# 64 unused bytes behind each of the first group's four T tiles: places that step by 64 modulo 256

## The chip, the cores and the metric

The kernel runs on one core of a Trainium2 chip. The metric is the time of one execution on the device, in microseconds. The profile is of one execution on the same core.

## What is computed

One step of a one-layer decoder trunk, for a prompt group of 1024 tokens and a sample group of 8 x 8 = 64 tokens with common weights, 1088 tokens in all, of width 1024, in float32:

```
h = RMSNorm(x)
q, k, v, gu, gv, ga, gb = split(h @ w_in)
A = sliding-window (128) grouped-query attention with per-head sinks
B = gelu(gu) * (W_s[g] LN(gelu(gv)) + b[g])      # 128-position chunks, W_s lower triangular
x = x + (sigmoid(ga) * (A @ w_branch_attn) + sigmoid(gb) * (B @ w_branch_gmlp)) @ w_out
z = RMSNorm(x) @ w_up                            # 1024 -> 2 * 2816
a, b = split(causal depthwise conv of width 3 over z)
x = x + (gelu(a) * b) @ w_down
y = RMSNorm(x)
```

Keys, values, the last rows of z and the normalised gv of the samples are outputs too.

## The kernel before

Every matrix product runs in float32r with both operands split in two: a high part that TensorE takes as it is, and the rest as a low part. A product is the sum of three matmuls, high x high, low x high and high x low. `split` (L39) makes the parts: a cast on ACT, a subtraction on DVE, both under L41.

The tokens stand in two groups. Group 0 has 576 (the 64 samples and 512 of the prompt), group 1 has 512. Two stages, the pair phase (L948, q, k, gu and the gates) and the up projection (L1570 and L1626), multiply pairs of weight tiles by the tokens with a scheme of seven products instead of eight: weights, tokens and outputs are cut into halves, seven sums of weight halves are multiplied by seven sums of token halves, and `Chain.product` (L293) adds or subtracts what comes out (L307 to L331). So for each of the two stages a group has seven sums of token halves for each of four pieces `kk` of the contraction, high and low: the T tiles.

Group 0's T tiles are made by `both_planes` (L258): one tile for each `kk`, 128 partitions x 7 sums x 2 planes (high, low) x 288 columns. `t0_job` (L657) fills them for the pair phase, in the pool `T0h`, and `t0_split` (L1421) for the up projection, in the pool `T0`. In the profile both are named `t`. Group 1's T tiles are separate tiles for high and low, 7 x 256 columns, in the pools `T1h` and `T1`; the profile names them `th` and `tl`.

One product of a chain is twelve matmuls into one PSUM bank, `st` (L305): for each `kk` the moving operand is the high plane with the weights' high part `wh`, the low plane with `wh`, and the high plane with their low part `wl`. Each loads its weights anew, 128 x 128. Where both groups are in work, a product of group 0 (288 columns) is followed by the same product of group 1 (256 columns) with the same weights. Three pairs of the pair phase and three of the up projection (`FEWA`, `FEW`) run on one group alone. The weights come through `Weights` (L72) from the pool `wp`, where each high or low part takes 8 pieces of 128 x 128.

Other stages that the prediction speaks of: `tokens` (L559, matmuls at L523), where the tokens are the weights and the projection's columns the moving operand (`w2h`, `w2l`); `mm3` (L231, matmuls at L238) for the branches and the output projection, with 320, 256 and 512 columns (`s`, `oh`, `ol`, `mh`, `ml`); and the down projection (L1673), with tiles `th`, `tl` of 544 columns taken as 288 and 256.

Pools are stacked from the two ends of on-chip memory. `line(pool, n)` (L246) takes a tile of n bytes for each partition that nothing reads or writes; the kernel has it already at other pools. `T0h` and `T0` are the first of the right side, from the upper end down. Below `T0h` lies `xr`, the staging for the pair phase's T tiles. Below `T0` lies `bt` (L1383): the group's rows `x1g`, `nacc` and two tiles `traw`, of which the sums of group 1's T tiles are made and split (L1491). When `bt` is closed, `c2` with the convolution's state `stc` is opened over its place and loaded by SP (L1595).

The order of the instructions on each engine is the order in which the code issues them, and waits come from the tiles' uses.

Of the kernel before, what the change touches and what calls it, by code (L numbers as in the profile page):

```python
# [34 lines left out]
def layer(tc, a):  # L35
# [13 lines left out]
    with ExitStack() as top:  # L49
# [196 lines left out]
        def line(pool, n):  # L246

            pool.tile([P, n // 4], F32, name=f"gap{next(gaps)}", bufs=1)
# [8 lines left out]

        def both_planes(pool, name):  # L258
            t = pool.tile([P, 7, 2, 288], F32R, name=name)
            return t[:, :, 0], t[:, :, 1]  # L260

        def combine(t4, b11, b12, b21, b22, eng=G):
# [108 lines left out]
        with ExitStack() as ph1:  # L371
# [285 lines left out]
            def t0_job(kk):  # L657
                def go():
                    first, t4, rest = sums_of(0, kk)
                    txa[0][kk] = th, tl = both_planes(t0h, f"t{kk}")  # L660
                    split(th[:, 0], tl[:, 0], first)
                    split(th[:, 1:5], tl[:, 1:5], t4)
                    split(th[:, 5:7], tl[:, 5:7], rest)
                return go
# [756 lines left out]
            def t0_split(kk):  # L1421

                def go():
                    x0, x1, t4 = hx.pop(kk)
                    tx[0][kk] = th, tl = both_planes(t0p, f"t0{kk}")
                    split(th[:, 0], tl[:, 0], x0[:, 0:288])
                    split(th[:, 5:7], tl[:, 5:7], x1.rearrange("p (h c) -> p h c", h=2))
                    split(th[:, 1:5], tl[:, 1:5], t4)
                return go
# [483 lines left out]
```

## Time and profile before

| | us |
|---|---|
| median of 3 runs | 1518.02 (1517.09 to 1523.28) |
| profiled execution | 1517.25 |
| its span, first to last instruction | 1515.5 |
| TensorE (PE) busy in the span | 1500.0 |
| weight loads (PEld) busy | 1459.7 |
| VectorE (DVE) busy | 1177.5 |
| ScalarE (ACT) busy | 848.7 |
| GpSimd (POOL) busy | 265.5 |

The mean granted clock of TensorE is 0.998. Weight loads overlap matmuls, and matmuls overlap one another: the duration of one runs from its first column to the end of its passage through the array, while the next one has long begun. The pace of a stream is therefore the distance from start to start, as the timeline shows it. In the lists of groups the columns are the line, the engine and the operation, output <- inputs by the program's names, the shape and the count, then busy time and the mean duration in ns of one, and the idle time before them. In the lists for one tile three numbers give the shortest, the median and the longest duration in ns.

### The profile page before, as it was taken

Reading aid. Unit: us, or ns where it says so; the run is one execution under the profiler, and the core shown is the slowest. Engines: PE = TensorE matmul, PEld = TensorE weight load, DVE = VectorE, ACT = ScalarE, POOL = GpSimd, SP = SyncE. Lnnn points to the kernel's source line nnn. Section 1 sums busy time; section 2 is a strip of 40 time slices with the busy share of each in tenths; the row PEclk is TensorE's granted clock in tenths of the full one; section 3 lists DMA queues with packets and bytes.
Section 4 is the critical chain, followed back from the end, with each engine's and each line's share of the span. In section 5 each row is a group of like instructions: output and inputs, shape, how many; then the busy total and the mean of one; then the engine's idle time right before and its main releaser. Section 6 shows DMA issues by size and latency. Waiting matters only on the chain.

```text
span 1515.5 us, 30104 instructions
## 1 busy us (share of the span) xinstructions
PE 1500.0 (99%) x11528; PEld 1459.7 (96%) x11528; DVE 1177.5 (78%) x1897; ACT 848.7 (56%) x1767; POOL 265.5 (18%) x382
## 2 busy tenths in 40 slices
PE   9999999999999999999999999999999999999997
PEld 9999999999998989988989999999999999999997
DVE  7799876755576877979568988898899888785686
ACT  7557676654465675764344555655555556353452
POOL 0001000110030222220134322332132222000002
PEclk9999999999999999999999999999999999999999
DMA  7688446864679757439988333332232216973463
GB/s 253 221 280 271 153 159 222 252 213 143 240 251 282 221 163 251 152 138 304 338 286 273 134 116 115 122 121 95 110 126 106 105 61 235 366 254 97 117 183 123
DMA packets 135231, 289.88 MB, mean 191 GB/s; under 512 B 15536, under 2 KB 36848, under 8 KB 135088
## 3 DMA queue, kind: packets, MB, share of 16 engines
q1 hardware_dynamic: 134944, 287.96, 56.4%
q8 instruction: 90, 1.47, 0.4%
q14 instruction: 53, 0.43, 0.1%
q10 hardware_dynamic: 144, 0.01, 0.0%
HBM read 198.97 MB, written 90.92 MB: 191 GB/s over the span
## 4 chain that ended last, share of the span: by engine, by line
PE 83%; DVE 6%; ACT 4%; DMA 3%; issue 2%; POOL 1%; SPq 0%; POOLq 0%; ACTq 0%; DVEq 0%
PE st L305 45%; PE dn L1673 13%; PE mm L238 13%; PE st L523 6%; PE po L1222 2%; PE sc L1171 1%; DVE wl L41 1%; PE pt L1198 1%; DMA v<-gvd 1%; ACT wh L41 1%; PE mx L805 1%; DMA vnd<-v 1%; ACT s L1188 1%; DMA kd<-q 0%; DVE tl L41 0%
## 5 line engine op out<-in xcount | busy, mean ns | idle before, releaser
L305 PE MATMUL st<-t,wh 128*128 128x288 f32 x2128 | 429.8, 294 | 0.8 <-ACT kn L286 0.8
L305 PEld LDWEIGHTS st<-t,wh 128*128 128x128 f32 x2128 | 337.3, 188 | 1.9 <-ACT kn L286 1.0
L305 PE MATMUL st<-t,wl 128*128 128x288 f32 x1064 | 314.2, 295 | 0.0
L305 PE MATMUL st<-th,wh 128*128 128x256 f32 x1064 | 297.9, 280 | 1.0 <-ACT k L284 0.9
L305 PE MATMUL st<-tl,wh 128*128 128x256 f32 x1064 | 296.3, 278 | 0.0
L305 PE MATMUL st<-th,wl 128*128 128x256 f32 x1064 | 295.1, 277 | 0.0
L305 PEld LDWEIGHTS st<-th,wh 128*128 128x128 f32 x1064 | 200.7, 189 | 2.3 <-ACT k L284 1.8
L305 PEld LDWEIGHTS st<-th,wl 128*128 128x128 f32 x1064 | 200.7, 189 | 0.0
L305 PEld LDWEIGHTS st<-t,wl 128*128 128x128 f32 x1064 | 200.2, 188 | 0.0
L305 PEld LDWEIGHTS st<-tl,wh 128*128 128x128 f32 x1064 | 199.8, 188 | 0.0
L1673 PE MATMUL dn<-th,wh 128*128 128x288 f32 (+1 forms) x616 | 176.9, 287 | 1.0 <-ACT zb L331 0.6
L1673 PE MATMUL dn<-tl,wh 128*128 128x288 f32 (+1 forms) x616 | 176.2, 286 | 0.0
L1673 PE MATMUL dn<-th,wl 128*128 128x288 f32 (+1 forms) x616 | 175.2, 284 | 0.2 <-DVE wl L41 0.2
L41 ACT CAST wh<-wraw 128x512 fp32r<-128x512 f32 (+2 forms) x188 | 129.5, 701 | 79.2 <-DMA wraw<-wt 27.0
L41 DVE TENSOR_TENSOR wl<-wraw,wh 128x512 fp32r<-128x512 f32 (+2 forms) x188 | 148.8, 804 | 28.0 <-ACT wh L41 25.7
L41 ACT CAST wh<-ws 128x512 fp32r<-128x512 f32 x168 | 102.5, 621 | 93.9 <-PE st L305 60.3
L41 DVE TENSOR_TENSOR wl<-ws,wh 128x512 fp32r<-128x512 f32 x168 | 117.8, 712 | 46.9 <-ACT wh L41 46.2
L1673 PEld LDWEIGHTS dn<-th,wh 128*128 128x128 f32 x616 | 115.6, 188 | 1.4 <-ACT zb L331 0.9
L1673 PEld LDWEIGHTS dn<-th,wl 128*128 128x128 f32 x616 | 115.9, 188 | 0.4 <-DVE wl L41 0.4
L1673 PEld LDWEIGHTS dn<-tl,wh 128*128 128x128 f32 x616 | 115.7, 188 | 0.0
L41 ACT CAST th<-traw 128x544 fp32r<-128x544 f32 (+1 forms) x85 | 54.6, 643 | 48.3 <-PE dn L1673 34.9
L523 PE MATMUL st<-w2h,hh 128*128 128x256 f32 x288 | 79.9, 279 | 0.9 <-ACT w2h L41 0.4
(275 smaller groups left out, 3181.8 us busy)
## 6 DMA issues: line engine op xcount, KB each, us to landing
wraw<-wt SPq DMA_DIRECT2D x137, 512.0 KB
traw<-td SPq DMA_DIRECT2D x77, 272.0 KB
td<-za SPq DMA_DIRECT2D x22, 544.0 KB
q<-qd SPq DMA_DIRECT2D x16, 512.0 KB
upd<-hl SPq DMA_DIRECT2D x14, 512.0 KB
td<-t SPq DMA_DIRECT2D x11, 544.0 KB
wpart<-wt SPq DMA_DIRECT2D x22, 256.0 KB
qd<-q SPq DMA_DIRECT2D x8, 576.0 KB
```

The source lines that it names most:

```text
L41: for x in (S.copy(hi, src), V.tensor_sub(lo, src, hi.bitcast(F32))):
L238: PE.matmul(ps[:, lo:lo + c1 - c0], u[:, k, :], v[:, c0:c1], start=(k == 0 and i == 0), stop=(k == nk - 1 and i == 2))
L305: PE.matmul(ps, u[:, kk, :], v, start=first and kk + i == 0, stop=kk == 3 and i == 2, skip_group_check=True)
L523: PE.matmul(ps, u[:, lo:lo + P], v[:, k, :], start=k + i == 0, stop=k == KD - 1 and i == 2)
L805: PE.matmul(ps[:, P * i:P * i + P], vn[:, i], late["wst"][:, c, :], start=True, stop=True)
L1171: PE.matmul(ps[:, h, o0:256], q, kst[kv][:, e, k0:cur + P], start=e == 0, stop=e == 1)
L1188: S.activation(s[:, h], s[:, h], AF.Exp, bias=nm[:, h:h + 1], accum_out=dn[:, h:h + 1])
L1198: PE.transpose(pt[:, h * P:h * P + P], s[:, h, 0:P], ident)
L1222: PE.matmul(po, v[:, kv, :], t, start=e == 0, stop=last)
L1673: PE.matmul(place(m, e), u[:, m, :], v[:, lo:hi], start=new and i + k == 0 and (e == 0 or m % 2 == 0), stop=i == NU - 1 and k == 2, skip_g ...
```

## The change

Behind each tile that `both_planes` makes, 64 bytes for each partition are left unused. `both_planes` is called by `t0_job` and by `t0_split`, so this holds in the pair phase and in the up projection.

```diff
         def both_planes(pool, name):
             t = pool.tile([P, 7, 2, 288], F32R, name=name)
+            line(pool, 64)
             return t[:, :, 0], t[:, :, 1]
```

`line` is as before:

```
        def line(pool, n):
            pool.tile([P, n // 4], F32, name=f"gap{next(gaps)}", bufs=1)
```

## The prediction

> **What bounds the kernel now.** I read the page first: the busy times, the chain that ended last, and the costliest groups.
>
> ```profile
> span 1515.5 us, 30104 instructions
> PE 1500.0 (99%) x11528; PEld 1459.7 (96%) x11528; DVE 1177.5 (78%) x1897; ACT 848.7 (56%) x1767; POOL 265.5 (18%) x382
> ...
> PE st L305 45%; PE dn L1673 13%; PE mm L238 13%; PE st L523 6%; PE po L1222 2%; PE sc L1171 1%; DVE wl L41 1%; PE pt L1198 1%; DMA v<-gvd 1%; ACT wh L41 1%; PE mx L805 1%; DMA vnd<-v 1%; ACT s L1188 1%; DMA kd<-q 0%; DVE tl L41 0%
> ...
> L305 PE MATMUL st<-t,wh 128*128 128x288 f32 x2128 | 429.8, 294 | 0.8 <-ACT kn L286 0.8
> ...
> L305 PE MATMUL st<-t,wl 128*128 128x288 f32 x1064 | 314.2, 295 | 0.0
> L305 PE MATMUL st<-th,wh 128*128 128x256 f32 x1064 | 297.9, 280 | 1.0 <-ACT k L284 0.9
> L305 PE MATMUL st<-tl,wh 128*128 128x256 f32 x1064 | 296.3, 278 | 0.0
> L305 PE MATMUL st<-th,wl 128*128 128x256 f32 x1064 | 295.1, 277 | 0.0
> ```
>
> PE is busy 99% of the span, and L305, the product of a chain, is 45% of the chain that ended last. So nothing has to be waited for less: the time changes if PE's matmuls follow each other at another pace, and hardly otherwise. The groups named `t` read the four T tiles of the first group: 2128 + 1064 = 3192 matmuls of 288 columns, twelve to a product (four tiles, three matmuls each), 266 products. Those named `th`, `tl` read the second group's tiles, 3 x 1064 = 3192 of 256 columns. The mean of one (294 ns) is not the pace, because matmuls overlap in the array. The pace stands in the timeline, from start to start. A product of both chains near the end of the up projection:
>
> ```profile
> 1236.35 0.28 PE L305 MATMUL st<-th,wh 128*128 128x256 f32 x1
> ...
> 1236.94 0.28 PE L305 MATMUL st<-th,wl 128*128 128x256 f32 x1
> ...
> 1237.62 0.28 PE L305 MATMUL st<-th,wl 128*128 128x256 f32 x1
> 1237.74 0.42 PE L305 MATMUL st<-t,wh 128*128 128x288 f32 x2
> ...
> 1239.19 0.29 PE L305 MATMUL st<-t,wl 128*128 128x288 f32 x1
> 1239.32 0.28 PE L305 MATMUL st<-th,wh 128*128 128x256 f32 x1
> ```
>
> The twelve matmuls on T tiles go from 1237.74 to 1239.32: 1.58 us, 132 ns each. All 3192 take 3192 x 0.132 = 421 us, 28% of the span. The twelve of the second group take 1237.74 - 1236.35 = 1.39 us. Their first five need 0.59 us, 118 each, the last seven (1236.94 to 1237.74) 0.80 us, 114 each. So a run of 256 columns starts slowly behind a run of 288 and then settles. The duration follows the pace, 294 at 132 and 276 at 113 to 114, always some 162 above it, so durations can be compared in place of paces. The spread by tile:
>
> ```profile
> L305 PE MATMUL st<-t,wh x2128: 290/294/401, 110.5 to 1259.9; 128*128 128x288 f32 x194
> ...
> L305 PE MATMUL st<-t,wl x1064: 290/295/298, 110.8 to 1260.0; 128*128 128x288 f32 x178
> ...
> L305 PE MATMUL st<-th,wh x1064: 276/276/387, 145.5 to 1271.4; 128*128 128x256 f32 x178
> ```
>
> Minimum, median, maximum: matmuls of one shape (the `wl` row, where none waited) go from 290 to 298. That is all there is for a change of places to move.
>
> **The change, part by part.** It adds a name without an instruction behind each T tile. Engine by engine, the built programs have the same instructions in the same order. A T tile is 7 x 2 x 288 x 4 = 16,128 bytes, 63 x 256, so all four begin at one place modulo 256, which in the built program is 224. The high plane of every product is at 224 (a step of 2304 bytes is 9 x 256), the low plane 1152 bytes on, at 96. The weights' `wh` and `wl` are at 32 for every tile. With 64 bytes more the tiles are at 224, 32, 96 and 160, their low planes at 96, 160, 224 and 32. Everything stacked below them (`xr`, `bt`) moves by 256 bytes and keeps its place modulo 256. Nothing else moves.
>
> *Pace of the 3192 matmuls of 288 columns.* No row shows them at 32 or 160. Bounds from the rows above: if each ran at the minimum, 290 in place of 294, the gain is 4 ns x 3192 = 12.8 us; at the maximum, 298 in place of 295, the loss is 3 x 3192 = 9.6 us. In between, the nearest rows are matmuls of the same shape at another place, and others whose place differs:
>
> ```profile
> L1673 PE MATMUL dn<-th,wh 128*128 128x288 f32 x308 | 91.5, 297 | 0.3 <-ACT wh L41 0.3
> L1673 PE MATMUL dn<-tl,wh 128*128 128x288 f32 x308 | 91.1, 296 | 0.0
> L1673 PE MATMUL dn<-th,wl 128*128 128x288 f32 x308 | 90.1, 292 | 0.2 <-DVE wl L41 0.2
> ...
> L1673 PE MATMUL dn<-tl,wh 128*128 128x256 f32 x308 | 85.1, 276 | 0.0
> ...
> L238 PE MATMUL mm<-mh,wl 128*128 128x512 f32 x64 | 24.9, 389 | 0.0
> ...
> L238 PE MATMUL mm<-oh,wl 128*128 128x320 f32 x64 | 19.9, 311 | 0.0
> ...
> L238 PE MATMUL mm<-mh,wl 128*128 128x320 f32 x64 | 19.7, 308 | 0.0
> ```
>
> In the down projection the 288 columns of both planes begin at 96: (297 + 296 + 292) / 3 = 295.0, against (2 x 294 + 295) / 3 = 294.3 here. The 320 columns of `oh` begin at 224 and those of `mh` at 96: 311 and 308, of which part is the fuller phase in which the former run. The 512 columns of `mh` begin at 32, the very place of the weights, and cost (389 - 276) / 256 = 0.44 ns for each column above 256, no more than the (389 - 308) / 192 = 0.42 above 320. So three places, 96, 224 and 32, show paces alike within 1 to 3 ns. I take 0, with 1 ns either way (3.2 us) as the likely error, and keep -12.8 and +9.6 as ends. The fourth place, 160, is shown for no stream with weights at 32.
>
> The Trainium skill speaks against any effect, in "SBUF — State Buffer", section "SBUF: two separate sides": "PE, ACT, and DVE's dedicated pair never wait on anyone." By it the sum is 0 here, as I take it. The trace neither shows that nor refutes it, but 290 to 298 for one shape at a granted clock of 1.00 is a spread for which the rule has no place. The skill's "TensorE: Matmul & The Clock Gate", section "Back-to-back issue gap", gives columns / 2.4 + 2.5 ns: 122.5 for 288 columns, an estimate 9.5 below the measured 132, or 30 us over 3192. Since no matmul of this shape here comes near it, it is not an end of the range.
>
> *Settling of the 256 columns behind them.* Settled is 276. The means 280, 278 and 277 give (4 + 2 + 1) x 1064 = 7.4 us that unsettled matmuls cost now. In the down projection 256 columns follow 288 too and run at 276 to 277 from the first on. So the gain can be 7.4. The other end is a run of 256 columns that never settles, which the token projection (L523) has, its operands at one place throughout:
>
> ```profile
> 70.00 0.28 PE L523 MATMUL st<-w2l,hh 128*128 128x256 f32 x1
> ...
> 71.42 0.28 PE L523 MATMUL st<-w2l,hh 128*128 128x256 f32 x1
> ...
> 428.00:451.00 23.00, 23.00 (x206) 1.00 0.88 311
> ```
>
> Twelve matmuls in 1.42 us, 118.3 each, while 23.0 us of the second group's alone hold 206, with both that reach over the edges (113 each). The cost would be (118.3 - 113.3) x 3192 = 16.0, less the 7.4 already paid: +8.6 us. I take 0: the matmul ahead of the run still ends in the same chain, and nothing in these rows says towards which end its new place pushes.
>
> *Two new waits.* The load of `stc` (L1595) now also waits for the last split of the second group's tiles, whose staging tile has moved 256 bytes down into it.
>
> ```profile
> 845.45 0.42 SPq L1595 DMA_DIRECT2D stc<-stc  x1
> 848.57 0.33 SPq L1584 DMA_DIRECT2D zd<-zb  x1
> ...
> 845.92 0.93 DVE L41 TENSOR_TENSOR tl<-traw,th 128x512 fp32r<-128x512 f32 x1
> ...
> 852.11 0.62 POOL L1566 COPY za<-stc 128x18 f32<-128x18 f32 x1 [4.58 <-DVE wl L41]
> ```
>
> The split ends at 846.85, so the issue goes from 845.45 to about 846.9. Behind it on SP stands the store of `zb` at 848.57, which waits for a later DVE instruction anyway, and the first reader on POOL comes at 852.11. Cost 0; if that cover were gone, 1.4 us. On POOL one later copy out of `za` (L1551) also waits for ACT, at a point where ACT's last use of the old tile is some 14 us past. Cost 0.
>
> **The sum.** The profiled execution took 1517.25 us, its span 1515.5 and 1.75 around it: 1517.25 + 0 + 0 + 0. The median of the runs is 1518.02, 0.77 higher, so I say 1518.0. The likely case's own range is the 3.2 us above with half the settling term (3.7): 1511 to 1525.
>
> **The rivals.** *The runs fall into step* (faster). A duration of 290 exists, as the minimum shows, and a regular step of places could keep it. In full that is 12.8 + 7.4 = 20.2 us, 1497.8; half of it, 1507.9. For it: all slower paces come without a named wait. Against it: 224, 96 and 32 look alike in the rows, and within a tile the two planes stay 128 apart, so the sequence remains irregular. It counts as faster from 7.6 us on, say all of the settling or 2.4 ns of each 288.
>
> *The second group's runs no longer settle* (slower). Place: the first 256 columns behind the fourth tile, which now ends at 160 + 1152, that is 32, and no longer at 96, modulo 256. Price +8.6, and with 1 ns on each 288 +3.2 more: 1518.0 + 11.8 = 1529.8. It decides as soon as the settling takes over eleven of twelve matmuls in place of five. For it: a run at 118 keeps itself up over dozens of matmuls at L523. Against it: in the down projection such runs settle at once, behind 288 columns at yet another place.
>
> *The change does nothing to PE*: the places matter to no engine, and the time is 1517.25 to 1518.02. That lies inside the forecast and has 0.2 of its chance.
>
> **How the numbers follow.** What a measurement of this kernel can tell from no change is about 0.5%, 7.6 us. Forecast (within that) 0.50; in step 0.24; not settling, or a slower pace of the 288 columns, 0.26. The range takes in the half of the faster rival and nearly all of the slower one: 1507 to 1529, with some 0.1 left out at either side.
>
> **What would show it.** Right: the `t` rows again at 294 and 295, the mean of `th,wh` at 280, twelve T matmuls in 1.58 us, the `stc` load 1.4 us later and POOL's first copy where it was. Faster would show as `t` rows near 290 or `th,wh` near 276; slower as `th` and `tl` rows near 281. I am wrong altogether if time appears at PE as idle time behind DVE, ACT or DMA, since no instruction has changed its order.

## The result and the profile after

The changed kernel takes 1513.39 us (median of 6 runs, 1511.22 to 1515.95), the kernel before beside it 1520.96 us (6 runs, 1517.09 to 1523.28). The ratio is 0.9953, with a 95% interval from 0.9936 to 0.9971: a gain of 4.4 to 9.7 us, which is small but is not nothing. The profiled execution took 1511.66 us.

The page of the kernel after, with the busy times and the costliest groups (busy us, mean ns of one, then idle time before them; a line added in `both_planes` makes L305 to L306):

```profile
span 1509.9 us, 30105 instructions
PE 1492.6 (99%) x11528; PEld 1452.6 (96%) x11528; DVE 1176.0 (78%) x1897; ACT 849.6 (56%) x1767; POOL 269.8 (18%) x382
...
L306 PE MATMUL st<-t,wh 128*128 128x288 f32 x2128 | 428.5, 294 | 2.3 <-ACT kn L287 1.7
...
L306 PE MATMUL st<-t,wl 128*128 128x288 f32 x1064 | 312.5, 294 | 0.0
L306 PE MATMUL st<-th,wh 128*128 128x256 f32 x1064 | 295.4, 278 | 0.7 <-ACT k L285 0.6
L306 PE MATMUL st<-tl,wh 128*128 128x256 f32 x1064 | 294.1, 276 | 0.0
L306 PE MATMUL st<-th,wl 128*128 128x256 f32 x1064 | 293.8, 276 | 0.0
```

The span is 5.6 us shorter and PE's busy time 7.4 us less, with as many matmuls. What became shorter are the rows of the **second** group, `th` and `tl`, whose tiles the change does not touch: 280, 278, 277 are now 278, 276, 276. The rows named `t`, whose tiles did move, went from 294 and 295 to 294 and 294.

The timeline of the kernel after shows how, in the same stretch of the up projection as in the prediction (start and duration in us):

```profile
1230.62 0.28 PE L306 MATMUL st<-th,wh 128*128 128x256 f32 x1
...
1231.19 0.28 PE L306 MATMUL st<-th,wl 128*128 128x256 f32 x1
...
1231.98 0.42 PE L306 MATMUL st<-t,wh 128*128 128x288 f32 x2
...
1233.43 0.29 PE L306 MATMUL st<-t,wl 128*128 128x288 f32 x1
1233.56 0.28 PE L306 MATMUL st<-th,wh 128*128 128x256 f32 x1
```

The first five of the second group's twelve now take 1231.19 - 1230.62 = 0.57 us, 114 each, where they took 0.59, 118 each. The last seven keep 0.79 (0.80 before). The first group's twelve take 1.58 us as before.

The timeline shows 10 ns; the trace has single ns. So below I count the **twelve** of a product from the start of its first matmul to the start of the next product, as a mean over all products in which nothing waited (some 204 of the first group behind one of the second, 218 the other way round). Before: 1580.9 and 1391.8 ns. After: 1576.7 and 1365.5 ns. Twelve settled matmuls of 256 columns take 1360. Summed over all start-to-start distances below 150 ns, the first group's matmuls take 418.1 us before and 416.8 after, the second group's 366.9 and 361.1: both chains together 785.1 and 778.0, 7.1 us less. The distances behind all other matmuls sum to 711.1 and 711.7 us, and the 41 longer ones within the chains to 11.4 and 12.3. So 7.1 us less and 0.6 and 0.9 more make the 5.6 us by which the span is shorter.

The new wait on SP stands in the timeline of the kernel after (SP's queue, DVE, POOL):

```profile
843.57 0.33 SPq L1595 DMA_DIRECT2D cw<-convw  x1
845.39 0.33 SPq L1596 DMA_DIRECT2D stc<-stc  x1
847.09 0.33 SPq L1585 DMA_DIRECT2D zd<-zb  x1
...
844.44 0.93 DVE L41 TENSOR_TENSOR tl<-traw,th 128x512 fp32r<-128x512 f32 x1
...
850.71 0.53 POOL L1567 COPY za<-stc 128x18 f32<-128x18 f32 x1 [4.67 <-DVE wl L41]
```

The load of `stc` now comes 1.82 us behind that of `cw` (0.40 before), as foretold: it waits for the split, which ends at 844.44 + 0.93 = 845.37. POOL's first copy still waits for DVE's `wl` (4.67 us, 4.58 before). These rows show no cost: the copy starts 5.3 us after the load is issued, released by the same instruction as before.

### The profile page after: what moved, and what is told of

Read it like the earlier page. It is cut to its first block, busy times and chain, and to the rows that moved or that the text cites. A ratio compares the mean times of both kernels' runs of the same rounds, so it can differ in the third digit from the quotient of the medians.

```text
span 1509.9 us, 30105 instructions
## 1 busy us (share of the span) xinstructions
PE 1492.6 (99%) x11528; PEld 1452.6 (96%) x11528; DVE 1176.0 (78%) x1897; ACT 849.6 (56%) x1767; POOL 269.8 (18%) x382
## 4 chain that ended last, share of the span: by engine, by line
PE 86%; DVE 5%; ACT 3%; issue 2%; DMA 2%; POOL 1%; SPq 0%; POOLq 0%; ACTq 0%; DVEq 0%
PE st L306 49%; PE dn L1674 13%; PE mm L238 13%; PE st L524 6%; PE po L1223 2%; PE sc L1172 1%; DVE wl L41 1%; PE pt L1199 1%; DMA stg<-sd 1%; PE mx L806 1%; ACT s L1189 1%; DVE tl L41 0%; ACT wh L41 0%; DMA x<-xt 0%; DVE wpart L460 0%
## 5 line engine op out<-in xcount | busy, mean ns | idle before, releaser
L306 PE MATMUL st<-t,wh 128*128 128x288 f32 x2128 | 428.5, 294 | 2.3 <-ACT kn L287 1.7
L306 PEld LDWEIGHTS st<-t,wh 128*128 128x128 f32 x2128 | 335.8, 188 | 3.0 <-ACT kn L287 1.9
L306 PE MATMUL st<-t,wl 128*128 128x288 f32 x1064 | 312.5, 294 | 0.0
L306 PE MATMUL st<-th,wh 128*128 128x256 f32 x1064 | 295.4, 278 | 0.7 <-ACT k L285 0.6
L306 PE MATMUL st<-tl,wh 128*128 128x256 f32 x1064 | 294.1, 276 | 0.0
L306 PE MATMUL st<-th,wl 128*128 128x256 f32 x1064 | 293.8, 276 | 0.0
L306 PEld LDWEIGHTS st<-th,wh 128*128 128x128 f32 x1064 | 199.8, 188 | 2.1 <-ACT k L285 1.6
L306 PEld LDWEIGHTS st<-t,wl 128*128 128x128 f32 x1064 | 199.8, 188 | 0.0
L306 PEld LDWEIGHTS st<-th,wl 128*128 128x128 f32 x1064 | 199.8, 188 | 0.0
L306 PEld LDWEIGHTS st<-tl,wh 128*128 128x128 f32 x1064 | 199.8, 188 | 0.0
```

What stands on the lines that cost most here:

```text
L306: PE.matmul(ps, u[:, kk, :], v, start=first and kk + i == 0, stop=kk == 3 and i == 2, skip_group_check=True)
```

## The experiments

The runs move tiles and leave every instruction as it is. Places are given as bytes **above the weights**, modulo 256: the weights are at 0, group 1's T tiles at 192, group 0's four T tiles at 192, 192, 192, 192 before the change and at 192, 0, 64, 128 after it. That is where the high plane begins; the low plane is 128 further on. The prediction and the expectations give the places themselves, with the weights at 32, so their 224, 32, 96 and 160 are 192, 0, 64 and 128 here. Modulo 256 is enough to tell streams apart here: the seven sums of a tile lie 9 x 256 bytes apart in group 0 and 4 x 256 in group 1, and 199 of the second group's 218 products before take 1392 to 1396 ns whichever sum they use.

A single execution of the kernel before took 1516.47 to 1519.86 us beside these runs, so a single time does not carry a verdict here; the pace of the twelve does.

Two theories stand against each other. By the first (S in the expectations), the **step** does it: four places in a regular order let the second group's run settle. By the second (P), the **last tile** does it: only the place of the fourth T tile, whose matmuls come right before the second group's, counts.

The seven kernels that move group 0's tiles have one edit and differ in its numbers:

```diff
         def both_planes(pool, name):
+            kk = int(name[-1])
+            if kk == 0 and T_GAPS[0]:
+                line(pool, T_GAPS[0])
             t = pool.tile([P, 7, 2, 288], F32R, name=name)
+            if T_GAPS[kk + 1]:
+                line(pool, T_GAPS[kk + 1])
...
+T_GAPS = (0, 0, 0, 192, 64)      # e1: 192, 192, 192, 128
+T_GAPS = (192, 0, 0, 0, 64)      # e2: 128, 128, 128, 128
+T_GAPS = (64, 64, 64, 64, 0)     # e3: 0, 64, 128, 192
+T_GAPS = (0, 0, 0, 128, 128)     # e4: 192, 192, 192, 64
+T_GAPS = (64, 0, 0, 0, 192)      # e7: 0, 0, 0, 0
+T_GAPS = (0, 32, 32, 32, 160)    # e8: 192, 224, 0, 32
+T_GAPS = (128, 0, 0, 0, 128)     # e9: 64, 64, 64, 64
```

First what these runs gave, one profiled execution each, then run by run:

| kernel | T tiles above the weights | first group's twelve, ns | second group's twelve, ns | both chains, us | time, us |
|---|---|---|---|---|---|
| before | 192 192 192 192 | 1580.9 | 1391.8 | 785.1 | 1517.25 |
| after | 192 0 64 128 | 1576.7 | 1365.5 | 778.0 | 1511.66 |
| e1 | 192 192 192 128 | 1588.3 | 1372.9 | 782.7 | 1516.58 |
| e2 | 128 128 128 128 | 1589.7 | 1364.5 | 780.2 | 1512.65 |
| e3 | 0 64 128 192 | 1585.0 | 1381.7 | 783.0 | 1519.42 |
| e4 | 192 192 192 64 | 1583.5 | 1366.2 | 779.9 | 1513.67 |
| e7 | 0 0 0 0 | 1616.0 | 1386.4 | 791.4 | 1523.90 |
| e8 | 192 224 0 32 | 1589.8 | 1382.6 | 785.9 | 1517.71 |
| e9 | 64 64 64 64 | 1594.2 | 1394.5 | 790.8 | 1524.74 |

**e1, the last tile alone at the place that it has in the change; e2, all four there, without a step; e3, a step, but ending where the tiles were before; e4, the last tile alone at another place.**

> Only the fourth T tile is moved, to 160 modulo 256; the first three stay at 224 (the 256 bytes of the pool are spent as 192 ahead of the fourth tile and 64 behind it). Theory P, that the pace of the second group's run is set by where the last matmul ahead of it stands: the run settles as in the changed kernel, th,wh / tl,wh / th,wl at means of 278 / 276 / 276 ns, span about 1510.5 us. Rival S, that it takes the step from tile to tile: means as before, 280 / 278 / 277, span about 1515.5 us.

> All four T tiles at 160 modulo 256, no step between them. P: the second group's run settles as in the changed kernel, 278 / 276 / 276 ns, span about 1510.5 us, 288 columns at 294. S: as before, 280 / 278 / 277, span about 1515.5 us.

> Tiles at 32, 96, 160 and 224 modulo 256: the same step of 64, but the fourth tile back at 224. P: the second group's run as before, 280 / 278 / 277 ns, span about 1515 us. S: as in the changed kernel, 278 / 276 / 276, span about 1510 us.

> Only the fourth T tile moved, to 96 modulo 256, so that its high plane ends at 224, where the second group's tiles begin, as in the down projection. P: the run settles at once, 276 to 277 ns in all three groups, up to 7.4 us less than before, span about 1508.5 us. S: as before, 280 / 278 / 277, span about 1515.5 us.

The groups on the page of e2, without a step:

```profile
L310 PE MATMUL st<-t,wh 128*128 128x288 f32 x2128 | 431.3, 296 | 2.0 <-ACT k L289 1.0
...
L310 PE MATMUL st<-t,wl 128*128 128x288 f32 x1064 | 312.9, 294 | 0.0
L310 PE MATMUL st<-th,wh 128*128 128x256 f32 x1064 | 295.3, 278 | 0.8 <-ACT k L289 0.6
L310 PE MATMUL st<-tl,wh 128*128 128x256 f32 x1064 | 294.0, 276 | 0.0
L310 PE MATMUL st<-th,wl 128*128 128x256 f32 x1064 | 293.8, 276 | 0.0
```

And on that of e3, with a step that ends at 192:

```profile
L310 PE MATMUL st<-th,wh 128*128 128x256 f32 x1064 | 297.2, 279 | 2.2 <-ACT k L289 2.1
L310 PE MATMUL st<-tl,wh 128*128 128x256 f32 x1064 | 295.2, 278 | 0.0
L310 PE MATMUL st<-th,wl 128*128 128x256 f32 x1064 | 294.8, 277 | 0.0
```

And on that of e4, where only the last tile is away from 192:

```profile
L310 PE MATMUL st<-th,wh 128*128 128x256 f32 x1064 | 295.4, 278 | 0.7 <-ACT k L289 0.6
L310 PE MATMUL st<-tl,wh 128*128 128x256 f32 x1064 | 294.2, 277 | 0.0
L310 PE MATMUL st<-th,wl 128*128 128x256 f32 x1064 | 293.9, 276 | 0.0
```

The theory of the step falls. e2 and e4 have none, and the second group settles as with the change: 278, 276, 276 in e2, twelve in 1364.5 and 1366.2 ns. e3 has one and keeps 22 of the 32 ns (1391.8 - 1360) that the settling cost before. In e3 the first four distances (medians) are 118, 120, 118 and 118 ns, with the change 116 and then 114. So the last tile's place decides most of it. It is not all: e1 has the last tile where the change has it, and its twelve take 1372.9 ns, 7.4 more, with a first distance of 122. What lay before the last tile counts too.

The first group's own twelve go the other way in e1 and e2: 1588.3 and 1589.7, 12 to 13 ns longer than with the change. So in these two runs the first group loses a part of what the second gains (it took 1580.9 before), and with the change it loses nothing.

**e7, all four at the weights' own place; e8, a step of 32; e9, all four at 64.**

> All four T tiles at 32 modulo 256, the place of the weights. P: the second group's run settles within about two matmuls, 278 / 276 / 276 ns, as with the last tile at 160 or 96; only 224 is slow. If a place equal to the weights' costs the 288 columns, t rows at 296 to 298, up to 9.6 us more; if not, 294 to 296.

> A step of 32 in place of 64: tiles at 224, 0, 32 and 64. P: the last tile is not at 224, so 278 / 276 / 276 ns for the second group, span 1509 to 1513 us. If only multiples of 64 give this, 280 / 278 / 277 and about 1515.

> All four T tiles at 96, 64 above the weights; the planes of a tile change roles against the kernel before (high at 64 above the weights, low at 192). If what ends the slow start of the second group's run is a last plane 64 or 128 above the weights: 278 / 276 / 276 ns and 1.365 us for twelve, as with the last tile alone at 96. If it takes a change of place between the third and the fourth tile: 280 / 278 / 277. The 288 columns between 294 and 296.

The groups on the page of e7:

```profile
L310 PE MATMUL st<-t,wh 128*128 128x288 f32 x2128 | 436.6, 298 | 1.4 <-ACT kn L291 0.9
...
L310 PE MATMUL st<-t,wl 128*128 128x288 f32 x1064 | 315.7, 297 | 0.0
L310 PE MATMUL st<-th,wh 128*128 128x256 f32 x1064 | 296.4, 279 | 1.1 <-ACT k L289 1.0
L310 PE MATMUL st<-tl,wh 128*128 128x256 f32 x1064 | 296.7, 279 | 0.0
L310 PE MATMUL st<-th,wl 128*128 128x256 f32 x1064 | 295.4, 278 | 0.0
```

At the weights' own place the first group's matmuls are at their slowest: 1616.0 ns for twelve, 134.7 each. Behind them the second group does not settle at once either (1386.4), although its forerunner is not at 192. In e8 the mean of 1382.6 hides two kinds: 154 products take 1369 to 1374 ns, and 64 never settle (1411 to 1420). So the expectation of both runs, that only 192 is slow, failed. In these runs the second group settles after one matmul with all four tiles at 128, with the change, or with the last alone at 64; it takes longer in the others. e9 limits even that. Its last tile is at 64 as in e4, yet the mean is 1394.5: about half of its products settle after a few matmuls (twelve in some 1377) and the others never do (some 1413), which neither of its two expectations had. Two products in a row of e9's timeline:

```profile
1228.80 0.28 PE L310 MATMUL st<-tl,wh 128*128 128x256 f32 x1
...
1230.09 0.43 PE L310 MATMUL st<-t,wh 128*128 128x288 f32 x2
...
1231.70 0.28 PE L310 MATMUL st<-th,wh 128*128 128x256 f32 x1
1231.82 0.28 PE L310 MATMUL st<-tl,wh 128*128 128x256 f32 x1
...
1233.08 0.43 PE L310 MATMUL st<-t,wh 128*128 128x288 f32 x2
```

From the second matmul on the first of them takes 1230.09 - 1228.80 = 1.29 us for eleven, 117.3 each to its end; the other 1233.08 - 1231.82 = 1.26, 114.5 each. The places of both are the same. The two kinds alternate with two kinds of the first group's products: one of some 1582 ns is followed by one of 1413 in all 106 cases, one of some 1608 by one of 1377 in all 94. So at fixed places the pace of a product goes with that of the product ahead; the runs do not show why.

**e6, everything at the left end of memory moved by 64 bytes.** The weights go from 32 to 96 and group 1's T tiles with them, group 0's stay. So the differences of the chains are those of e2, at other places.

```diff
+        line(W.pool, 64)
         tx = [{}, {}]
```

> All pools of the left side moved by 64 bytes, with them the weights (to 96) and the second group's tiles (to 32), while the first group's T tiles stay at 224: every place relative to another is that of the run with all four tiles at 160. If only differences modulo 256 count, the chains are as there: t,wh 296, t,wl 294, th 278 / 276 / 276 ns, twelve T matmuls behind a run of the second group 1.59 us. If the place itself counts, they are as before, 294 / 295 / 280 / 278 / 277. The token projection also gets operands at other places (both at 224), so its time may move by itself.

The groups on the page of e6:

```profile
L306 PE MATMUL st<-th,wh 128*128 128x256 f32 x1064 | 295.3, 278 | 0.7 <-ACT k L285 0.6
L306 PE MATMUL st<-tl,wh 128*128 128x256 f32 x1064 | 294.0, 276 | 0.0
L306 PE MATMUL st<-th,wl 128*128 128x256 f32 x1064 | 293.8, 276 | 0.0
```

The chains are those of e2 almost to the ns: 1589.7 and 1364.8 for twelve, 780.2 us in all, and the twelve medians of the first group differ by 1 ns at one place. So it is the places relative to each other that count, and the paces repeat from one execution to another. The whole took 1523.13 us all the same, since other streams changed their differences. From the lists of groups by shape of e6, where the distances behind all other matmuls are 719.1 in place of 711.1 us:

```profile
L1674 PE MATMUL dn<-th,wl 128*128 128x256 f32 x308 | 86.8, 282 | 0.0
L1674 PE MATMUL dn<-tl,wh 128*128 128x256 f32 x308 | 86.5, 281 | 0.0
L1674 PE MATMUL dn<-th,wh 128*128 128x256 f32 x308 | 86.3, 280 | 0.8 <-ACT zb L332 0.8
L524 PE MATMUL st<-w2h,hh 128*128 128x256 f32 x288 | 81.6, 285 | 0.6 <-ACT rst L490 0.4 <-ACT hh L46 0.2
L524 PE MATMUL st<-w2l,hh 128*128 128x256 f32 x288 | 81.1, 282 | 0.0
L524 PE MATMUL st<-w2h,hl 128*128 128x256 f32 x288 | 80.4, 282 | 0.2 <-DVE hl L47 0.2
```

In the down projection the 256 columns went from 192 to 128 above their weights (and the 288 columns ahead of them from 64 to 0), and from 277, 276, 276 to 280, 281, 282: 14 ns x 308 = 4.3 us. In the token projection the moving operand went from 192 to 0 above the first group's tokens, which are the weights there, and the rows rise from 279, 278 and 278 by 6, 4 and 4 ns: 14 x 288 = 4.0 us. From start to start each of the two stages is 4.0 us longer, and together they are the 8 us. The first group's tokens, at 0, run at 120.0 ns for long stretches. The second group's tokens kept their 192, but not their pace: from 85 to 115 us the median duration is 281, where it was 276.

**e5, e10, e11, group 1's T tiles of the up projection at 128, 64 and 0 above the weights, and not at 192; group 0's as before the change.**

```diff
-        line(t1p, 192)
+        line(t1p, 128)      # e5;  e10: line(t1p, 64);  e11: line(t1p, 256)
```

> The first group's T tiles as in the kernel before, all at 224; the second group's tiles of the up projection at 160 in place of 224 (128 unused bytes ahead of them, not 192); the pair phase untouched. Theory R, that what counts is the place of the last T tile against the place of the run that follows: in the up projection the twelve matmuls of the second group now take 1.37 us, in the pair phase 1.39 as before, th,wh at a mean of 279 ns over both. Rival W, that what counts is a stream's place against the weights' alone: a fourth T tile at 224 still gives 1.39 us in both, and the second group's settled matmuls may leave 276 ns for up to 281.

> First group's T tiles as before at 224; the second group's tiles of the up projection at 96, 64 above the weights. If only the place 128 above the weights keeps runs of 256 columns from settling, they settle at 276 again in the up projection and th rows stay at 277 to 280; if 192 above is the only place where they settle, the up projection's twelve take 1.41 us or more, th rows at 280 to 281.

> As the run before it, but the second group's tiles of the up projection at 32, the weights' own place. If a place equal to the weights' costs most, as it did the 288 columns (1.616 us for twelve, 0.035 more than at 224), the twelve of 256 take 1.42 us or more and the th rows stand above 281; if it is neutral, 277 to 280.

The timelines of one stretch in which the second group runs alone, before (15 matmuls from the first row to the second):

```profile
970.55 0.28 PE L305 MATMUL st<-th,wh 128*128 128x256 f32 x1
...
972.25 0.28 PE L305 MATMUL st<-th,wh 128*128 128x256 f32 x1
```

e5, 36 matmuls:

```profile
979.04 0.28 PE L305 MATMUL st<-th,wh 128*128 128x256 f32 x1
...
983.36 0.28 PE L305 MATMUL st<-th,wh 128*128 128x256 f32 x1
```

e10, 21 matmuls:

```profile
970.33 0.28 PE L305 MATMUL st<-th,wh 128*128 128x256 f32 x1
...
972.80 0.28 PE L305 MATMUL st<-th,wh 128*128 128x256 f32 x1
```

e11, 21 matmuls:

```profile
974.24 0.28 PE L305 MATMUL st<-th,wh 128*128 128x256 f32 x1
...
976.76 0.28 PE L305 MATMUL st<-th,wh 128*128 128x256 f32 x1
```

Before, 15 in 1.70 us are 113.3 each. e5: 36 in 4.32 us, 120.0 (118.3 a little earlier in the same stretch; over all its products alone 1430.8 / 12 = 119.2). e10: 21 in 2.47 us, 117.6 (1412.9 / 12 = 117.7 over all). e11: 21 in 2.52 us, 120.0. Nothing stands ahead of these matmuls but their like, nothing waits, and the clock granted in these stretches is 1.00. So at these places the stream is slow by itself, and not only behind the first group.

But a place alone does not fix the pace. In e9 the second group's tiles are at 192 as before, and where this group runs alone in the pair phase, its timeline shows

```profile
438.09 0.28 PE L310 MATMUL st<-th,wh 128*128 128x256 f32 x1
...
439.86 0.28 PE L310 MATMUL st<-th,wh 128*128 128x256 f32 x1
```

These are 15 matmuls in 1.77 us, 118.0 each, where the same stage before has 113.3. Twenty products in a row there take 1412 to 1414 ns, which is the pace of e10 at 64. The stretch of the token projection in the prediction (118.3 each, 117.8 from single ns) is at 192 too. So at 192 a stream runs at 113.3 or, less often, at 117.8. At 64, 128 and 0 no product of the second group alone took less than 1409, 1420 and 1429 ns. 192 is the only one of the four at which 113.3 was read, and 120.0 over whole products stands only at 128 and 0. Each of e5, e10 and e11 is one execution.

Behind the first group the twelve take 1419.4, 1413.1 and 1435.8 ns there (1392.1 before, in the same stage): the prediction's slower rival, brought about in another way. Both numbers that e5's expectations gave for them, 1.37 and 1.39 us, were too low; that settled matmuls may leave 276 ns came true. For e10 and e11 the slower of the two expectations came true.

**e12, the change and the same step for the output projection's tiles of group 0.**

```diff
             hl = tuple(hmp[g].tile(...))
+            if g == 0:
+                line(hmp[0], 64)
```

> The change, and beside it 64 unused bytes behind each high and low tile of the first group in the output projection (mh, ml: 384 matmuls of 320 and 256 columns, now 308 and 279 ns, a pair of the two widths every 263 ns), so that their places step by 64 modulo 256. If a step helps any stream that alternates its widths, the mh and ml rows of 320 and 256 columns go to about 304 and 276 ns: 192 pairs by 4 ns are 0.8 us, and at most 1.6 us if both widths settle. If only the place of the last tile ahead of a settled run counts, there is no settled run to come to here, the rows stay at 308 and 279, and the time is that of the change alone. Either way the whole time is 0.994 to 0.997 of the kernel before, which 5 rounds should show apart from 1, with the t rows at 294 and th rows at 278, 276, 276 as with the change.

The list of groups by shape of e12:

```profile
L238 PE MATMUL mm<-mh,wh 128*128 128x320 f32 x64 | 19.8, 309 | 0.0
L238 PE MATMUL mm<-ml,wh 128*128 128x320 f32 x64 | 19.7, 308 | 0.0
...
L238 PE MATMUL mm<-mh,wl 128*128 128x256 f32 x64 | 18.0, 280 | 0.0
```

The rows stay at 308 to 309 and go from 279 to 280. The time is 1513.41 us (12 runs, 1510.16 to 1518.44) against 1519.07 for the kernel before (16 runs), ratio 0.996, interval 0.9946 to 0.9974: the change's own effect again, and nothing from the edit. The chains repeat, in another execution, what the change gave: 1576.8 and 1365.3 ns for twelve, 778.0 us. Streams whose widths alternate at every matmul do not settle here by a step of 64. No placement tried gives less than the change's 778.0 us for the two chains.

## Why the prediction was right, and where it was not

**The forecast.** It said 1518.0, a difference that measurement cannot tell, and 1507 to 1529. The time fell by 0.47%, which is inside the 0.5%, though at its edge, and the runs do show a difference. So the forecast held, but its sum of 0 was mis-sized by some 7 us: 7.1 by the two chains, 7.6 by the medians. That it held is in part luck: the prediction's faster rival counts from 7.6 us on, the medians differ by 7.57, and the interval reaches 9.7. Its own sign, `th,wh` again at 280, failed: it is 278, halfway to the 276 of the faster rival.

**Pace of the 288 columns: 0, with 3.2 us as the likely error.** It held: 418.1 to 416.8 us, -1.3. The argument behind it, that 96, 224 and 32 show paces alike within 1 to 3 ns, held for this shape: all four tiles at 192, 128, 64 or 0 above the weights give 131.7, 132.5, 132.9 and 134.7 each. It doesn't carry over to other shapes. That the 512 columns at the weights' place cost no more for each column was true of those rows, but the 256 columns of e11 cost 6.7 ns more there than at 192.

**Settling of the 256 columns: taken as 0, with ends at -7.4 and +8.6.** This is the term that was mis-sized. It measured -5.8 us (366.9 to 361.1), or by the prediction's own rows (2 + 2 + 1) x 1064 = -5.3: most of the gain that the bound allowed. The sentence that failed is "nothing in these rows says towards which end its new place pushes". One row pointed to the gain, though for another new place. The down projection's 288 columns begin 64 above the weights, and its 256 columns 1152 bytes on, at 192, just where the second group's T tiles are. The second stream is in the same place in both stages, and it settles at once behind 64 but not behind 192. The prediction used that row as an end of the range and as an argument against the slower rival, and did not read it as a case in which, of the places, only the forerunner's differs (the runs there are of six matmuls, not twelve). e4, with its last tile at 64, is that case made in the chains: 1366.2. For 128, the place of the change, no row was there.

**The two waits: 0.** Right for the load of `stc`, as its rows show: issued 1.4 us later, and POOL's copy released by the same instruction as before. POOL's later copy out of `za` (L1552 after) waited for DVE's `za` in 21 cases, as before, and in none was ACT what ended the wait.

**The rivals.** "The runs fall into step" came true in one half and failed in the other. The settling went most of the way that its full case has it, but not through a step: e2 and e4 give it without one, and e3 has a step and does not. The 4 ns on each matmul of 288 columns did not come: the minimum is 290 still, and no placement brought the mean of their twelve below 1576.7 ns. The distances within a product vary from place to place, before as after (medians of 128 to 134 ns), so the shortest duration was no pace that all twelve could keep. "The second group's runs no longer settle" went the other way. Its point that an unsettled run keeps itself up was sound: e9, e10 and e11 have such runs, at 117 to 120 ns. What it had wrong was the placement that brings them about. "The change does nothing to PE" is refuted, by e2 against e1 as much as by the change, since both have the same instructions in the same order.

**The Trainium skill's rule** that PE never waits for another engine at on-chip memory ("SBUF — State Buffer", "SBUF: two separate sides") gave 0, and the chains measured -7.1 us. No view here can tell whether PE is held up there by another engine, so the rule is neither shown nor refuted; it has no place for a pace that moves with where PE's own two operands lie, and the runs show that: 113.3 ns before and 117.7 to 120.0 in e5, e10 and e11, for one shape in a steady stream. The formula that the prediction takes from "TensorE: Matmul & The Clock Gate", section "Back-to-back issue gap", is given there by the Trainium skill for an isolated matmul, with no time for the load of its weights. So the measured 132 ns, of a stream with a load for each matmul, do not contradict its 122.5.

**What stays open.** The runs show that the places count, relative to each other, and which are good. They don't show why. With the second group's tiles always at 192 above the weights while the first group's moved, the runs can't say whether the last tile's place counts against the weights or against the tile that follows. Nor do they say why e1 settles less well than the change, what decides between 113.3 and 117.8 ns at 192, or whether a stream at 64 can reach 113.3 at all.

## What to carry to other kernels

Where PE is busy 99% of the time and waits for nothing, read the pace of its matmuls from start to start and compare streams of one shape by their places modulo 256, each operand against its weights and against the stream ahead of it: 6% of the pace (113.3 to 120.0 ns) can lie there, with no idle time to show it. Read many products and more than one execution, since 4% can come and go at one placement. A gap that mends one stream moves others (e6: 5 us gained in the chains, 8 lost elsewhere), so put it where nothing else shifts, and look at every group. When a row serves as a bound, ask as well what in it differs from the case at hand: where that is nearly one thing only, it is an experiment already made.

## What the runs showed of the hardware that was not expected

A steady stream of float32r matmuls of 256 columns, each with new weights, takes 113.3 or 117.8 ns each with its moving operand 192 bytes above the weights modulo 256 (before and e9). At 64 it takes 117.7 (e10), at 128 a mean of 119.2 (e5), at 0 120.0 (e11). The token projection in e6 agrees at 0, with other tiles: in the stretch from 30 to 55 us its median duration is 283 ns where it was 276.

At one and the same placement two paces can both last: 113.3 and 117.8 at 192, 118.4 and 120.0 in e5. In e9 products of the two kinds alternate.

The pace of a stream's first matmuls goes with where the stream ahead of it lay. Before, with all four tiles at 192, the first five distances are 118 to 123 ns. With all four at 128 (e2), or the last alone at 64 (e4), one is 116 and the next 114.
